# Attention weights transposed on DVE and by DMA through DRAM, in place of TensorE

## The chip, the cores and the metric

The kernel runs on one core of a Trainium2 chip. The metric is the device time of one execution in microseconds. Besides it the profile gives the span, from the first to the last instruction of the profiled execution.

The engines are named as in the profile: PE is TensorE's matmul, PEld its weight load, DVE is VectorE, ACT ScalarE, POOL GpSimd, and SP the engine that issues nearly all DMAs (SPq in the rows). L345 is line 345 of the kernel before.

## The reference

Two layers, on 256 tokens of width 2048, all float32. Each layer normalises the input, projects it to queries, keys and values, and runs two groups of eight attention heads on it. Then come an output projection and an MLP of width 8192. Cut to what the change touches:

```python
# (A) differential heads, 8 of value width 128, global:
p = jax.nn.softmax(sc, axis=-1)
w = (p[:, :, 0] - lam * p[:, :, 1]).astype(v.dtype)
return jnp.einsum('bhqk,bkhe->bqhe', w, v)
# (B) neighbourhood heads, 8 of width 128, window of 4 rows x 16 columns on a 64-wide grid, with bias:
p = jax.nn.softmax(sc.reshape(b, h, GRID_W, kr * kc), axis=-1).reshape(b, h, GRID_W, kr, kc)
return jnp.einsum('bhcrj,brcjhd->bchd', p.astype(v.dtype), v_nb)
```

The kernel computes (B) densely, with a mask: for each head the weights are a matrix of 256 queries by 256 keys. Both kinds of head need it with the keys on the partitions, since the product with v sums over keys.

## The kernel before

The weights of the whole model are a stream of 384 slabs of 128 x 2048 numbers (1 MB), 192 a layer. The program walks through them in order. For each slab SP loads `raw` (three buffers). ACT then writes the rounded high half `whi`, and DVE the rest `wlo`, in two pieces of 1024 columns each (lines 154 and 155; four buffers of either, so two slabs). PE multiplies a slab in one of two ways. `block_product` (lines 177 to 179) does 24 matmuls of 512 columns. `wide_product` does 16 of 512 columns (line 204) and 16 of 256 (line 208).

Attention is laid between the slabs. A head is a Python generator that stands in a list of tasks; `yield n` gives way for n slabs, and `between_slabs` wakes it. This sets priorities; a scheduler then lays out each engine's order of instructions, and at run time each engine works through its list in order and waits on semaphores.

- `diff_head` (16 in the program): scores, maxima (line 388), exponentials on ACT (line 391), the weighted difference `wd` on DVE (line 400), two slabs' pause, four transposes on PE (line 345), a copy from PSUM on ACT (line 405), one slab's pause, product with v (line 353).
- `na_head` and `na_stages` (16): two wide products give q and k of one head, so a head is reached every two slabs. Then scores (lines 439 to 441), bias (line 444), maxima (line 448), exponentials (line 452), division by the sum (line 457), two slabs' pause, four transposes (line 345), a split of the result into high half on ACT (line 325) and rest on DVE (line 326), one slab's pause, product with v in six matmuls (lines 465 to 467). The neighbourhood heads of a layer are called head 0 to head 7 below.

Each of the 32 heads thus has four PE transposes of 128 x 128, against an identity matrix, into one PSUM tile of the tag `tp` (two buffers). All slab loads go to SP in program order (line 71).

Of the kernel before, what the change touches and what calls it, by code (L numbers as in the profile page):

```python
# [12 lines left out]
F32 = mybir.dt.float32  # L13
F32R = mybir.dt.float32r
AF = mybir.ActivationFunctionType
# [4 lines left out]
P = 128  # L20
D = 2048
S = 256
NT = S // P
# [13 lines left out]
NB = 512  # L37
NEG = -1.0e30
IDLE = 9
RUN = 5 * RPB_C + GRID_W  # L40

RPB_FIRST = RPB_HEAD - 1 - (10 * RPB_C + GRID_W - 1 + WIN_C - 1)
# [8 lines left out]
def body(ctx, tc, x, x_t, w, gains_in, gains_o, final_g, lam_in, rpb, ident_in, rope_in, mask_in, out):  # L51
    nc = tc.nc
# [3 lines left out]
    work = ctx.enter_context(tc.tile_pool(name="work", bufs=2))  # L56
    small = ctx.enter_context(tc.tile_pool(name="small", bufs=4))
    ps = ctx.enter_context(tc.tile_pool(name="ps", bufs=2, space=PSUM))


    gin = const.tile([P, 2 * DEPTH, NK], F32, name="gin")
# [4 lines left out]
    go = const.tile([P, DEPTH, HEADS + 1], F32, name="go")  # L66
    xs = [const.tile([P, D], F32, name=f"x{t}") for t in range(NT)]

    def stream(dst, src):

        tc.keep_in_program_order(nc.sync.dma_start(dst, src))

    lam_sb = [None]

# [56 lines left out]
            between_slabs()  # L131


    slab_no = [0]
    x_rest = [None]

    def next_slab():
# [199 lines left out]
        nc.scalar.activation(rb, pb, AF.Copy)  # L337
        return rb

    def transposed_weights(pr):  # L340

        pw = ps.tile([P, NT, S], F32, name="tp", tag="tp", bufs=2)
        for t in range(NT):
            for kt in range(NT):
                nc.tensor.transpose(pw[:, kt, t * P:(t + 1) * P], pr[:, t, kt * P:(kt + 1) * P], ident)  # L345
        return pw

    def weights_times_v(wt, v, j):

# [26 lines left out]
    def diff_head(q, k, vs, j, nlam, gsub, put):  # L376

        neg = small.tile([P, 2, NT], F32, name="neg")
        sm = small.tile([P, 2, NT], F32, name="sm")
        pr = []  # L380
        sc = [ps.tile([P, NT, S], F32, name="sc", tag="sc", bufs=2) for _ in range(2)]
        for t in range(NT):
            for m in range(2):
                both = q[m][:, j, t * P:(t + 1) * P]
                nc.tensor.matmul(sc[m][:, t, :], both, k[m][:, j, :], start=True, stop=False)  # L385
                nc.tensor.matmul(sc[m][:, t, :], both, k[2 + m][:, j, :], start=False, stop=True)  # L386
        for m in range(2):
            nc.vector.tensor_reduce(neg[:, m, :], sc[m], axis=AX.X, op=ALU.max, negate=True)
            p = work.tile([P, NT, S], F32, name="pr", tag="pr", bufs=3)
            for t in range(NT):  # L390
                nc.scalar.activation(p[:, t, :], sc[m][:, t, :], AF.Exp, bias=neg[:, m, t:t + 1],
                                     accum_out=sm[:, m, t:t + 1])
            pr.append(p)
        rs = small.tile([P, 2, NT], F32, name="rs")
        nc.vector.reciprocal(rs, sm)
        c = small.tile([P, NT], F32, name="c")
        nc.vector.scalar_tensor_tensor(c, sm[:, 0, :], nlam, rs[:, 1, :], op0=ALU.mult, op1=ALU.mult)
        wd = work.tile([P, NT, S], F32, name="wd", tag="wd")
        for t in range(NT):
            nc.vector.scalar_tensor_tensor(wd[:, t, :], pr[1][:, t, :], c[:, t:t + 1], pr[0][:, t, :],  # L400
                                           op0=ALU.mult, op1=ALU.add)
        yield 2
        pw = transposed_weights(wd)
        wt = work.tile([P, NT, S], F32, name="wT", tag="wT", bufs=3)
        nc.scalar.activation(wt, pw, AF.Copy)
        yield 1
        po = weights_times_v(wt, vs[0], j)
        ss = small.tile([P, NT], F32, name="sso")
        for t in range(NT):
            junk = work.tile([P, HD], F32, name="junk", tag="junk", bufs=1)  # L410
            nc.scalar.activation(junk, po[:, t, :], AF.Square, scale=rs[:, 0, t:t + 1],
                                 accum_out=ss[:, t:t + 1])
        r = rms_scale(ss, NT, HD)
        comb = small.tile([P, NT], F32, name="comb")
        nc.gpsimd.tensor_tensor(comb, r, rs[:, 0, :], op=ALU.mult)
        o = work.tile([P, NT, HD], F32, name="o", tag="o", bufs=4)
        for t in range(NT):
            nc.vector.tensor_scalar(o[:, t, :], po[:, t, :], comb[:, t:t + 1], None, op0=ALU.mult)
        yield 2
        put(to_mix(o, gsub))  # L420
# [14 lines left out]
    def na_stages(h, q, k, v, rq, bias, gain, sq_sum, put):  # L435
        sc = ps.tile([P, NT, S], F32, name="sc", tag="sc", bufs=2)
        for t in range(NT):
            ts = slice(t * P, (t + 1) * P)
            nc.tensor.matmul(sc[:, t, :], q[0][:, ts], k[0], start=True, stop=False)  # L439
            nc.tensor.matmul(sc[:, t, :], q[1][:, ts], k[0], start=False, stop=False)  # L440
            nc.tensor.matmul(sc[:, t, :], q[0][:, ts], k[1], start=False, stop=True)
        sb = work.tile([P, NT, S], F32, name="wd", tag="wd")
        for t in range(NT):
            nc.vector.scalar_tensor_tensor(sb[:, t, :], sc[:, t, :], rq[t],
                                           bias[:, 2 - 2 * t:6 - 2 * t, :].rearrange("p a b -> p (a b)"),
                                           op0=ALU.mult, op1=ALU.add)
        neg = small.tile([P, NT], F32, name="neg")
        nc.vector.tensor_reduce(neg, sb, axis=AX.X, op=ALU.max, negate=True)
        pr = work.tile([P, NT, S], F32, name="pr", tag="pr", bufs=3)
        sm = small.tile([P, NT], F32, name="sm")  # L450
        for t in range(NT):
            nc.scalar.activation(pr[:, t, :], sb[:, t, :], AF.Exp, bias=neg[:, t:t + 1],
                                 accum_out=sm[:, t:t + 1])
        rs = small.tile([P, NT], F32, name="rs")
        nc.vector.reciprocal(rs, sm)
        for t in range(NT):
            nc.scalar.activation(pr[:, t, :], pr[:, t, :], AF.Copy, scale=rs[:, t:t + 1])
        yield 2
        wt = split_plain(transposed_weights(pr), [P, NT, S], "wT", 3)
        yield 1  # L460
        po = ps.tile([P, S], F32, name="tp", tag="tp", bufs=2)
        j = h % 4
        for kt in range(NT):
            vh, vl = (part[:, kt, j * HD:(j + 1) * HD] for part in v)
            nc.tensor.matmul(po, vh, wt[0][:, kt, :], start=kt == 0, stop=False)  # L465
            nc.tensor.matmul(po, vl, wt[0][:, kt, :], start=False, stop=False)  # L466
            nc.tensor.matmul(po, vh, wt[1][:, kt, :], start=False, stop=kt == NT - 1)
        if h == 0:
            nc.scalar.activation(sq_sum, po, AF.Square)
        else:  # L470
            sq = work.tile([P, S], F32, name="sq", tag="o", bufs=4)
            nc.scalar.activation(sq, po, AF.Square)
            nc.gpsimd.tensor_tensor(sq_sum, sq_sum, sq, op=ALU.add)
        put(split_mix(po, gain))
# [225 lines left out]
```

## Time and profile before

| | us |
|---|---|
| median of 3 runs (2220.17 to 2221.09) | 2220.28 |
| the profiled execution | 2220.29 |
| its span | 2218.5 |
| PE busy | 2206.3 |
| PEld busy | 1884.7 |
| DVE busy | 1371.9 |
| ACT busy | 1121.7 |
| POOL busy | 91.7 |

An engine's busy time is the time in which it had an instruction under way. Matmuls overlap each other on PE, so what an instruction costs is read from the distance between starts rather than from its own length. Between the profiled execution and its span lie 1.8 us.

### The profile page before, as it was taken

What the parts mean: (1) busy time and instruction counts of PE and PEld (TensorE: products, weight loads), DVE (VectorE), ACT (ScalarE), POOL (GpSimd) and SP (SyncE); (2) the same over time, 40 slices, a digit from 0 to 9 for tenths busy, and PEclk for the clock granted to TensorE, in tenths of its full rate; (3) what the DMA queues carried; (4) which work ended last, traced back from release to release, by engine and by line L of the source; (5) the groups of instructions that cost most, each with busy time, mean ns of one, the idle gap of its engine ahead of it and who ended that gap; (6) DMA issues with size and microseconds to landing.
All of it is one profiled execution on the core that took longest, in us unless ns stands there. A gap on an engine that the chain in (4) does not pass through costs nothing.

```text
span 2218.5 us, 28803 instructions
## 1 busy us (share of the span) xinstructions
PE 2206.3 (99%) x11298; PEld 1884.7 (85%) x11298; DVE 1371.9 (62%) x1777; ACT 1121.7 (51%) x1677; POOL 91.7 (4%) x136
## 2 busy tenths in 40 slices
PE   9999999999999999999999999999999999999998
PEld 7888888888888888888888888888888888888886
DVE  7776765664565565565567767666655655655654
ACT  6665664544453454454456666545434434544543
POOL 1110110000000000000011101000000000000000
PEclk9999999999999999999999999999999999999999
DMA  9444445455555555555654444554555555555553
GB/s 330 172 171 163 163 168 182 180 189 192 196 190 191 201 188 190 192 190 190 199 180 168 171 166 158 189 186 178 189 193 198 188 192 194 190 190 190 190 190 133
DMA packets 61431, 414.31 MB, mean 187 GB/s; under 512 B 7024, under 2 KB 9328, under 8 KB 12144
## 3 DMA queue, kind: packets, MB, share of 16 engines
q1 hardware_dynamic: 60864, 411.40, 51.9%
q8 instruction: 88, 1.44, 0.3%
q10 hardware_dynamic: 432, 1.08, 0.1%
q14 instruction: 47, 0.39, 0.1%
HBM read 410.35 MB, written 2.10 MB: 186 GB/s over the span
## 4 chain that ended last, share of the span: by engine, by line
PE 99%; DMA 0%; ACT 0%; DVE 0%; POOL 0%; SPq 0%; issue 0%; ACTq 0%; POOLq 0%
PE accw L204 26%; PE acc L177 18%; PE acc L178 18%; PE acc L179 18%; PE accw L208 14%; PE tp L353 1%; PE tp L345 1%; PE tp L252 0%; PE sc L386 0%; PE sc L385 0%; PE tp L292 0%; DMA xT<-in_x_t 0%; PE tp L466 0%; PE sc L440 0%; PE tp L465 0%; PE sc L439 0%
## 5 line engine op out<-in xcount | busy, mean ns | idle before, releaser
L155 DVE TENSOR_TENSOR wlo<-raw,whi 128x1024 fp32r<-128x1024 f32 (+1 forms) x772 | 931.8, 1225 | 594.0 <-ACT whi L154 442.1
L154 ACT ACTIVATE whi<-raw 128x1024 fp32r<-128x1024 f32 (+1 forms) x772 | 813.5, 1055 | 855.4 <-PE acc L178 557.8
L204 PE MATMUL accw<-hT,whi 128*128 128x512 f32 x2560 | 614.1, 391 | 0.0
L204 PEld LDWEIGHTS accw<-hT,whi 128*128 128x128 f32 x2560 | 469.8, 188 | 90.5
L178 PE MATMUL acc<-whi,u2T 128*128 128x512 f32 x1024 | 399.0, 390 | 0.0
L177 PE MATMUL acc<-whi,u2T 128*128 128x512 f32 x1024 | 398.6, 389 | 0.0
L179 PE MATMUL acc<-wlo,u2T 128*128 128x512 f32 x1024 | 398.3, 389 | 0.0
L208 PEld LDWEIGHTS accw<-hT,wlo 128*128 128x128 f32 x2560 | 328.5, 191 | 12.5
L208 PE MATMUL accw<-hT,wlo 128*128 128x256 f32 x2560 | 332.4, 283 | 0.0
L179 PEld LDWEIGHTS acc<-wlo,u2T 128*128 128x128 f32 x1024 | 192.3, 188 | 39.8
L177 PEld LDWEIGHTS acc<-whi,u2T 128*128 128x128 f32 x1024 | 192.3, 188 | 39.5
L178 PEld LDWEIGHTS acc<-whi,u2T 128*128 128x128 f32 x1024 | 192.3, 188 | 39.3
L177 PE MATMUL acc<-whi,hT 128*128 128x512 f32 x512 | 201.6, 394 | 2.0 <-ACT whi L154 2.0
L178 PE MATMUL acc<-whi,hT 128*128 128x512 f32 x512 | 201.2, 393 | 0.0
L179 PE MATMUL acc<-wlo,hT 128*128 128x512 f32 x512 | 197.7, 392 | 0.0
L161 DVE SCALAR_TENSOR_TENSOR u2T<-u,u2T 128x256 fp32r<-128x256 f32 x128 | 54.3, 424 | 123.2 <-ACT u2T L160 123.2
L211 ACT ACTIVATE low<-accw 128x256 f32<-128x256 f32 x160 | 61.0, 381 | 124.3 <-PE accw L208 124.3
L177 PEld LDWEIGHTS acc<-whi,hT 128*128 128x128 f32 x512 | 96.3, 188 | 21.1 <-ACT whi L154 2.7
L179 PEld LDWEIGHTS acc<-wlo,hT 128*128 128x128 f32 x512 | 96.1, 188 | 19.3
L178 PEld LDWEIGHTS acc<-whi,hT 128*128 128x128 f32 x512 | 96.3, 188 | 18.4
L177 PE MATMUL acc<-whi,mix 128*128 128x512 f32 x256 | 101.0, 395 | 0.0
L178 PE MATMUL acc<-whi,mix 128*128 128x512 f32 x256 | 100.3, 392 | 0.0
(119 smaller groups left out, 1349.3 us busy)
## 6 DMA issues: line engine op xcount, KB each, us to landing
raw<-in_w SPq DMA_DIRECT2D x382, 1024.0 KB, 4.8
x<-in_x SPq DMA_DIRECT2D x2, 1024.0 KB, 11.2
out<-xg SPq DMA_DIRECT2D x8, 256.0 KB, 3.1
table<-in_rpb SPq DMA_DIRECT2D x4, 438.0 KB, 11.8
xT<-in_x_t SPq DMA_DIRECT2D x3, 512.0 KB, 8.6
raw<-in_w SPq DMA_DIRECT2D x4, 256.0 KB, 5.4
raw<-in_w SPq DMA_DIRECT2D x2, 512.0 KB, 7.6
gb<-in_final_g ACTq DMA_DIRECT2D x2, 512.0 KB, 4.4
```

Of the source, the lines that this page charges most:

```text
L154: nc.scalar.activation(hi[:, c:c + step], r, AF.Copy)
L155: nc.vector.tensor_sub(lo[:, c:c + step], r, hi[:, c:c + step].bitcast(F32))
L161: nc.vector.scalar_tensor_tensor(dst_lo, src, scale, dst_hi.bitcast(F32), op0=ALU.mult, op1=ALU.subtract)
L177: nc.tensor.matmul(acc[t], ah, wh, start=k == 0, stop=False)
L178: nc.tensor.matmul(acc[t], al, wh, start=False, stop=False)
L179: nc.tensor.matmul(acc[t], ah, wl, start=False, stop=k == n_k - 1)
L204: nc.tensor.matmul(acc, hi[:, (k % 8) * P:(k % 8 + 1) * P], h_t[k].rearrange("p a b -> p (a b)"), start=k == 0, stop=False)
L208: nc.tensor.matmul(acc[:, :S], lo[:, (k % 8) * P:(k % 8 + 1) * P], h_t[k][:, 0], start=False, stop=k == NK - 1)
L211: nc.scalar.activation(low, acc[:, S:], AF.Copy)
L345: nc.tensor.transpose(pw[:, kt, t * P:(t + 1) * P], pr[:, t, kt * P:(kt + 1) * P], ident)
L353: nc.tensor.matmul(po[:, t, :], wt[:, kt, t * P:(t + 1) * P], v[:, kt, j * HD:(j + 1) * HD], start=kt == 0, stop=kt == NT - 1)
```

## The change

The transposes leave PE. DVE's transpose instruction transposes each 32 x 32 square of the 128 x 512 tile within its own 32 partitions, into `sqt`. One DMA writes `sqt` to a DRAM tile `way` (256 KB). Four DMAs read it back into `moved`, each 64 KB: load `a` takes, for the 32 queries of one square row, four runs of 128 numbers (512 bytes) from each of the 32 rows and puts them on 4 x 32 partitions. The result has the keys on the partitions, and the query squares in the order a, t, u (which of four squares in a half, which half of the queries, which half of the keys).

The differential heads put this in order with two ACT copies (in place of one copy from PSUM). The neighbourhood heads split it as it lies, and PE reads the moving operand in runs of 32 numbers. A pause of one slab stands between the DVE transpose and the DMAs. Slab loads after the eighth are no longer held in program order. The tags change: `sqt` 2 buffers, `way` 4, `moved` 2, and `wT` or its two halves 2.

```diff
     def stream(dst, src):
 
-        tc.keep_in_program_order(nc.sync.dma_start(dst, src))
+        load = nc.sync.dma_start(dst, src)
+        if slab_no[0] < 8:
+            tc.keep_in_program_order(load)
...
-    def transposed_weights(pr):
-
-        pw = ps.tile([P, NT, S], F32, name="tp", tag="tp", bufs=2)
-        for t in range(NT):
-            for kt in range(NT):
-                nc.tensor.transpose(pw[:, kt, t * P:(t + 1) * P], pr[:, t, kt * P:(kt + 1) * P], ident)
-        return pw
+    def squares_transposed(pr):
+
+
+        sq = work.tile([P, NB // SQ // 4, NT, NT, SQ], F32, name="sqt", tag="sqt", bufs=2)
+        nc.vector.transpose(sq.rearrange("p b t u j -> p (t u) b j"),
+                            pr.rearrange("p t (u b j) -> p (t u) b j", u=NT, j=SQ))
+        return sq
+
+    def squares_moved(sq):
+
+
+        way = dram.tile([P, NB], F32, name="way", tag="way", bufs=4)
+        nc.sync.dma_start(way, sq.rearrange("p b t u j -> p (b t u j)"))
+        wt = work.tile([P, P // SQ, NT, NT, SQ], F32, name="moved", tag="wT", bufs=2)
+        for a in range(P // SQ):
+            nc.sync.dma_start(wt[:, a].rearrange("p t u j -> p (t u j)"),
+                              way[a * SQ:(a + 1) * SQ].rearrange("i (b e) -> b i e", b=P // SQ))
+        return wt
...
+        sq = squares_transposed(wd)
+        yield 1
+        moved = squares_moved(sq)
         yield 2
-        pw = transposed_weights(wd)
-        wt = work.tile([P, NT, S], F32, name="wT", tag="wT", bufs=3)
-        nc.scalar.activation(wt, pw, AF.Copy)
+        wt = work.tile([P, NT, S], F32, name="wT", tag="wTs", bufs=2)
+        for t in range(NT):
+            nc.scalar.activation(wt[:, :, t * P:(t + 1) * P].rearrange("p u (a j) -> p a u j", j=SQ),
+                                 moved[:, :, t], AF.Copy)
         yield 1
...
+        sq = squares_transposed(pr)
+        yield 1
+        moved = squares_moved(sq)
         yield 2
-        wt = split_plain(transposed_weights(pr), [P, NT, S], "wT", 3)
+        wt = split_plain(moved, [P, P // SQ, NT, NT, SQ], "wTs", 2)
         yield 1
...
-            nc.tensor.matmul(po, vh, wt[0][:, kt, :], start=kt == 0, stop=False)
-            nc.tensor.matmul(po, vl, wt[0][:, kt, :], start=False, stop=False)
-            nc.tensor.matmul(po, vh, wt[1][:, kt, :], start=False, stop=kt == NT - 1)
+            wh, wl = (part[:, :, :, kt, :].rearrange("p a t j -> p t a j") for part in wt)
+            nc.tensor.matmul(po, vh, wh, start=kt == 0, stop=False)
+            nc.tensor.matmul(po, vl, wh, start=False, stop=False)
+            nc.tensor.matmul(po, vh, wl, start=False, stop=kt == NT - 1)
```

How the change moves instructions is shown at three places, all among the neighbourhood heads of the first layer. Lines of the changed kernel are a little higher than those of before (L154 there is L159, L204 is L209, L325 is L330, L457 is L477, L465 is L489).

On PE before, at the end of a slab (line 208), the four transposes of head 4 stand ahead of the scores of head 5:

```order
L208 MATMUL accw<-hT,wlo 128x256 x16
L345 MATMUL tp<-ident,pr 128x128 x4
L439 MATMUL sc<-half 128x256
L440 MATMUL sc<-half 128x256
L441 MATMUL sc<-half 128x256
```

On PE after the change, at the end of that same slab (counting from 0 it is slab 46), stands the product with v of head 4 (L489 to L491, whose two `half` are the split weights):

```order
L209 MATMUL accw<-hT,whi 128x512 x16
L213 MATMUL accw<-hT,wlo 128x256 x16
L489 MATMUL tp<-half,vs 128x256
L490 MATMUL tp<-half,vs 128x256
L209 MATMUL accw<-hT,whi 128x512 x6
L491 MATMUL tp<-half,vs 128x256
L489 MATMUL tp<-half,vs 128x256
```

No transpose is left there; the product has moved back by one slab, to where the transposes stood.

On ACT before, the split of head 2's weights (`half_2554`, read from the PSUM tile `tp_2549`), then the exponentials and the division of head 3 (`pr_2570`):

```order
L325 ACTIVATE half_2554<-tp_2549 128x512
L325 ACTIVATE half_2544<-whole_2542 128x256
L154 ACTIVATE whi_2728<-raw_2726 128x1024
L452 ACTIVATE pr_2570,sm_2571<-wd_2565,neg_2568 128x256 x2
L154 ACTIVATE whi_2732<-raw_2726 128x1024
L457 ACTIVATE pr_2570<-pr_2570,rs_2574 128x256 x2
```

On ACT after the change, the split of head 2 (now read from `moved_2539`, the tile that the DMAs fill) and the division of head 3 (`pr_2620`):

```order
L330 ACTIVATE half_2684<-moved_2539 128x512
L159 ACTIVATE whi_2849<-raw_2847 128x1024
L472 ACTIVATE pr_2620,sm_2621<-wd_2615,neg_2618 128x256 x2
L159 ACTIVATE whi_2853<-raw_2847 128x1024
L330 ACTIVATE half_2678<-kr_2595 128x256
L477 ACTIVATE pr_2620<-pr_2620,rs_2624 128x256 x2
```

And a little further on, still on ACT after the change, the split of head 3 (`moved_2690`) and the division of head 4 (`pr_2772`):

```order
L472 ACTIVATE pr_2772,sm_2773<-wd_2767,neg_2770 128x256 x2
L159 ACTIVATE whi_3000<-raw_2998 128x1024
L330 ACTIVATE half_2836<-moved_2690 128x512
L477 ACTIVATE pr_2772<-pr_2772,rs_2776 128x256 x2
L159 ACTIVATE whi_3004<-raw_2998 128x1024
```

What moved: the split of a head, which waited for PE before, now waits for DMAs, and it stands ahead of the division by which the next head's weights become ready.

On SP before, the loads of the whole program are slabs, but for a few constants and the bias tables (`table`):

```order
L71 DMA lam_sb<-in_lam_in 128x512
L71 DMA go<-in_gains_o 128x18
L71 DMA negmask<-in_mask_in 128x64
L71 DMA table<-in_rpb 64x8x219 x2
L71 DMA raw<-in_w 128x2048 x185
L71 DMA table<-in_rpb 64x8x219 x2
```

On SP after the change, heads 3 and 4 (`sqt_2628` and `sqt_2780`) between the slabs:

```order
L75 DMA raw_3085<-in_w 128x2048
L357 DMA way_2688<-sqt_2628 128x512
L360 DMA moved_2690<-way_2688 128x1x128 x4
L75 DMA raw_3152<-in_w 128x2048
L357 DMA way_2840<-sqt_2780 128x512
L75 DMA raw_3220<-in_w 128x2048
L360 DMA moved_2842<-way_2840 128x1x128 x4
L75 DMA table_9596<-in_rpb 64x8x219
```

Five DMAs a head now stand in SP's list. At some heads a slab's load lies between the write of `way` and the four reads, at others not; the second layer's bias table has moved up into the first layer.

## Rows read from the trace of the kernel before

**Rows 1.** The page's parts 1 (busy time) and 4 (chain that ended last).
```profile
PE 2206.3 (99%) x11298; PEld 1884.7 (85%) x11298; DVE 1371.9 (62%) x1777; ACT 1121.7 (51%) x1677; POOL 91.7 (4%) x136
...
PE 99%; DMA 0%; ACT 0%; DVE 0%; POOL 0%; SPq 0%; issue 0%; ACTq 0%; POOLq 0%
```

**Rows 2.** Waits of all engines: us in total, times, longest us.
```profile
ACT whi L154 <- PE acc L178: 557.8, 350, 2.4
...
ACT whi L154 <- DMA raw<-in_w: 3.2, 3, 1.6
```

**Rows 3.** Groups by line, PE: xcount | busy us, mean ns of one | idle before.
```profile
L345 PE MATMUL tp<-ident,wd 128*128 128x128 f32 x64 | 9.9, 272 | 0.0
...
L345 PE MATMUL tp<-ident,pr 128*128 128x128 f32 x64 | 9.6, 272 | 0.0
```

**Rows 4.** Timeline of PE, heads 3 to 5, first layer: start us, us, instructions.
```profile
281.21 3.80 PE L204 MATMUL accw<-hT,whi 128*128 128x512 f32 x16
...
286.76 0.60 PE L345 MATMUL tp<-ident,pr 128*128 128x128 f32 x4
...
287.32 0.28 PE L440 MATMUL sc<-half 128*128 128x256 f32 x1
287.44 0.28 PE L441 MATMUL sc<-half 128*128 128x256 f32 x1
...
294.19 3.80 PE L204 MATMUL accw<-hT,whi 128*128 128x512 f32 x16
...
299.74 0.49 PE L345 MATMUL tp<-ident,pr 128*128 128x128 f32 x3
```

**Rows 5.** Timeline: slabs 26 and 37 on DVE, slab 27 on PE.
```profile
159.91 1.23 DVE L155 TENSOR_TENSOR wlo<-raw,whi 128x1024 fp32r<-128x1024 f32 x1 [0.26 <-ACT whi L154]
...
175.55 0.39 PE L177 MATMUL acc<-whi,hT 128*128 128x512 f32 x1
...
228.52 2.36 DVE L155 TENSOR_TENSOR wlo<-raw,whi 128x1024 fp32r<-128x1024 f32 x2 [0.49 <-PE accw L208]
```

**Rows 6.** Groups by line, ACT and DVE: xcount | busy us, mean ns of one.
```profile
L154 ACT ACTIVATE whi<-raw 128x1024 fp32r<-128x1024 f32 (+1 forms) x772 | 813.5, 1055 | 855.4 <-PE acc L178 557.8 <-PE accw L204 268.7 <-issue 13.4
...
L211 ACT ACTIVATE low<-accw 128x256 f32<-128x256 f32 x160 | 61.0, 381 | 124.3 <-PE accw L208 124.3
...
L452 ACT ACTIVATE pr<-wd,neg 128x256 f32<-128x256 f32 x32 | 16.0, 500 | 0.3
L457 ACT ACTIVATE pr<-pr,rs 128x256 f32<-128x256 f32 x32 | 14.4, 496 | 0.8 <-DVE rs L455 0.8
...
L448 DVE TENSOR_REDUCE neg<-wd 128x2 f32<-128x512 f32 x16 | 10.8, 677 | 0.1
...
L325 ACT ACTIVATE half<-tp 128x512 fp32r<-128x512 f32 x16 | 9.5, 593 | 0.6
...
L325 ACT ACTIVATE half<-kr 128x256 fp32r<-128x256 f32 x16 | 6.4, 401 | 1.6 <-DVE kr L426 1.6
L452 ACT ACTIVATION_READ_ACCUMULATOR pr<-wd,neg 128x1 f32 x32 | 6.0, 186 | 0.0
```

**Rows 7.** DMA queue (packets, MB, share) and issues: KB each, median us to landing.
```profile
q1 hardware_dynamic: 60864, 411.40, 51.9%
...
raw<-in_w SPq DMA_DIRECT2D x382, 1024.0 KB, 4.8
...
out<-xg SPq DMA_DIRECT2D x8, 256.0 KB, 3.1
table<-in_rpb SPq DMA_DIRECT2D x4, 438.0 KB, 11.8
...
xT<-in_x_t SPq DMA_DIRECT2D x1, 128.0 KB, 2.5
ident<-in_ident_in SPq DMA_DIRECT2D x1, 64.0 KB, 7.6
```

**Rows 8.** Tile `table`, its loads on SP: ns of an issue, min/median/max.
```profile
L71 SPq DMA_DIRECT2D table<-in_rpb x4: 596/622/714, 26.1 to 1084.4; - x4
```

More of the change, by code (lines that the diff above doesn't have):

```diff
@@ L39 @@
 IDLE = 9
+SQ = 32
 RUN = 5 * RPB_C + GRID_W
@@ L58, in body @@
     ps = ctx.enter_context(tc.tile_pool(name="ps", bufs=2, space=PSUM))
+    dram = ctx.enter_context(tc.tile_pool(name="dram", bufs=4, space=bass.MemoryType.DRAM))
     gin = const.tile([P, 2 * DEPTH, NK], F32, name="gin")
@@ L67, in body @@
     xs = [const.tile([P, D], F32, name=f"x{t}") for t in range(NT)]
+    slab_no = [0]
     def stream(dst, src):
-        tc.keep_in_program_order(nc.sync.dma_start(dst, src))
+        load = nc.sync.dma_start(dst, src)
+        if slab_no[0] < 8:
+            tc.keep_in_program_order(load)
     lam_sb = [None]
@@ L131, in finish_tasks @@
             between_slabs()
-    slab_no = [0]
     x_rest = [None]
```

## The prediction

> **What bounds the kernel now.** I read the page's busy times and the chain that ended last first [rows 1]. PE is busy for 2206.3 of the 2218.5 us of the span and makes 99% of the chain, DMA 0%. A share near 100% can still hide an engine that is slow at its own work, so the waits come next [rows 2]: ACT, which prepares the weights, stands idle 557.8 us in 350 waits until PE has finished with a buffer, and only 3.2 us for a slab that has not arrived. The stream of weights runs ahead of PE, so PE is the bound. What leaves PE leaves the time, one for one, as long as PE finds nothing new to wait for. The rest of the work is about that condition.
>
> **What is removed.** There are 64 transposes of `wd` and 64 of `pr` [rows 3]. Their busy time, 9.9 + 9.6 = 19.5 us, counts overlaps twice, so I take the distance between starts [rows 4]. From the start of four transposes (286.76) to the start of L440 (287.32) is 0.56 us, and L440 to L441 shows that a matmul of 256 columns takes 0.12. (L439, which stands between them in the program, has no row of its own here; it gets 0.12 as well.) Four transposes therefore cost 0.56 - 0.12 = 0.44 us, and 32 heads 32 x 0.44 = 14.1 us. Against the profiled execution's 2220.29, which is the median to within 0.01, that makes **2206.2**, if all else is hidden. The busy time, 19.5, is the gain's upper end: 2200.8.
>
> **What is added beside PE.** DVE gets 32 transposes of 128 x 512. No row shows one. The nearest is the reduction over the same 512 numbers, 0.68 us [rows 6]; I take 0.7, with twice that as the upper bound, together 22 to 45 us on an engine that is idle 38% of the span [rows 1]. A bound from below, nothing, would change no result. ACT's differential copy becomes two (at most 0.4 us each [rows 6], before one of about 0.6), the neighbourhood split keeps its size. Both are small against ACT's 557.8 us of waiting. Without that cover they would cost at most 32 x 0.7 = 22 us. PE now reads the neighbourhood weights in runs of 32. Between nothing and double the time for each of the 16 x 6 matmuls, 96 x 0.12 = 11.5 us, I take nothing: no row shows an operand read in such runs, so none speaks for a loss and none excludes it; it is rival C. The DMAs add 32 x 0.5 MB, 16.8 MB to 411.4 [rows 7], at a mean load of 51.9%. The issues cost 0.62 us each [rows 8], 3.1 us a head on SP, where the wait for `way` also holds the slab loads behind it. A slab lands in 4.8 us [rows 7], and heads are two slabs apart, so both together leave SP free over half the 12.98 us between two wide products [rows 4].
>
> At one place the notes speak against the change. The Trainium skill ("VectorE: DVE Perf Modes", The three transpose paths) says that DVE transposes only 32 x 32 blocks, and sends a full 128 x 128 one to TensorE. No run here has yet timed the alternative; here TensorE is the engine that bounds, which the rule does not weigh, and the sum by it would be no gain at all, 2220.
>
> **The new wait.** Call C the time from the end of the DVE transpose to the last landing of `moved`. It has three parts. `way`, 256 KB, lands in 3.1 us as `out` does, or 4.8 behind a slab. Three more issues follow the first read, 3 x 0.62 = 1.9. The last read, 64 KB, lands in 2.5 (`xT`, 128 KB), 4.8 (a slab), or 7.6 (`ident`, the same 64 KB, at the start of the program); 11.8 is the extreme (`table`) [rows 7, 8]. The lower end is 3.1 + 1.9 + 2.5 = 7.5, the upper 4.8 + 1.9 + 7.6 = 14.3, with the table's landing 18.5. I take one leg behind a slab and the other like `out`: 4.8 + 1.9 + 3.1 = 9.8, and 0.1 for each of three hand-overs (an estimate, from the 0.26 and 0.49 us that DVE waited for ACT and PE in [rows 5]): **C = 10.1**.
>
> Differential heads. The tightest is the first of the second block. DVE ends slab 26 at 159.91 + 1.23 = 161.1, the transpose 161.8, and PE reaches the product with v, ahead of slab 27's end, at 175.55 [rows 5]. Less 0.8 for the two copies, C may be 13.0. These are covered at 10.1.
>
> Neighbourhood heads. The order shows a ring that was not there before: on ACT the split of head h, which waits for `moved`, stands ahead of the division of head h + 1, without which that head's transpose and DMAs cannot begin. If C is long, the heads follow each other at C plus ACT's and DVE's work between, and no longer at PE's pace. That work, from [rows 6], with 0.59 for the split, 0.38 `low`, 0.69 an exponential with its accumulator, 1.06 a `whi`, 0.40 the half of k, about 0.9 to 1.0 the two divisions, 0.7 the transpose:
> head 0 to 1: split, low, divisions, transpose: 2.6; 1 to 2: split, low, two exponentials, whi, divisions, transpose: 5.0; 2 to 3: split, two whi, two exponentials, half, divisions, transpose: 6.1; 3 to 4: split, divisions, transpose: 2.2. Together 15.9.
> Head 0's transpose ends at 228.52 + 2.36 + 0.7 = 231.6, behind the two `wlo` of slab 37 [rows 5]. Head 4's product can start after five times C: 231.6 + 15.9 + 5C + 0.6 for its own split = 248.1 + 5C. On PE it stands where head 4's neighbour had its transposes, at 299.74 [rows 4], less five groups of 0.44 saved on the way: 297.5. So the ring is hidden up to **C = 9.9**, and each us beyond it costs 5 us a layer; the loop ends with the eighth head, whose limit I find about the same. At my C of 10.1 it gives back 1.0 us a layer: 2206.2 + 2.0 = **2208.2**. Behind the waiting split stand ACT's `whi` and, on DVE, `wlo` of the next slabs: they are the way by which a late head would stop PE.
>
> **Rivals.** *The trip through DRAM sets the pace (A).* The same sum with a longer C: the whole gain is gone at (14.1 / 2) / 5 = 1.4 us over the limit, C = 11.3, and beyond that the kernel is slower. At 14.3 it is 2206.2 + 2 x 5 x 4.4 = 2250. For it speaks that `ident` needed 7.6 us for 64 KB and that SP's list puts a slab's load between at some heads; against it that DMA is idle half the time and that `out` and `xT` landed in 3.1 and 2.5.
>
> *The reads are narrow (B).* Each read has a slowest dimension of four runs. If only four of the 16 DMA engines carry it, those four must move 128 packets a head besides their share of two slabs, 51.9% of 12.98 = 6.7 us. Two slabs take 12.98 - 0.44 = 12.5 us without the transposes, so the stream follows those four once the packets take over 12.5 - 6.7 = 5.8 us a head, 45 ns each; below that nothing is lost. By bytes, 51.9% x 2218.5 x 16 / 411.4 = 44.8 engine-us a MB [rows 1, 7], a head's 64 KB an engine is 2.9 us and hidden; by packets, 51.9% x 2218.5 x 16 / 60864 = 0.30 us each, it is 38.7 and ruinous. Packets of 512 bytes are much nearer the first price. With 10 us it would be about 2206.2 + 16 x (10 + 6.7 - 12.5) = 2273. The Trainium skill ("DMA: Bandwidth & Descriptors", Why a DMA increments its semaphore by 16 and not by 1) says that the number of engines is the largest one up to 16 that divides the slowest dimensions of both patterns, which here is 4; no run here shows it yet.
>
> *Reading runs of 32 slows PE (C):* 2206.2 + 11.5 = 2217.7, no difference to be told. *The transposes cost their busy time (D):* 2200.8.
>
> **How the numbers follow.** The ring's limit about met, as forecast, 0.55, itself from 2203 to 2214 (0.44 is read to 0.05 a group, and C to 0.8 on the far side). A 0.24: about 0.06 of it still faster, 0.07 with no difference, 0.11 slower. B slower 0.12, C 0.05, D 0.04. A measurement here can tell about 0.2%, 4.4 us, from no change. Faster: 0.55 + 0.06 + 0.04 = 0.65; same: 0.07 + 0.05 = 0.12; slower: 0.11 + 0.12 = 0.23. I predict the likeliest, 2208. From 2202 to 2236 the range leaves out D (0.04) and what of A and B lies beyond C = 12.9, some 0.15.
>
> **What would show it.** Right: no transposes on PE, PE busy down by 14 to 20 us, PE still 99% of the chain, `moved` landing soon enough that `split <- DMA moved` waits on ACT stay hidden, SP waiting for `way` some 3 to 5 us a head without slabs coming late. Ring: in the neighbourhood heads PE waits for the ACT half of the weights or for a `whi`, ACT waits for DMA `moved`, and the time between two wide products is over 12.5 us there and nowhere else. B: long DMA landings of `moved` and of the slabs beside it, and ACT waiting for `raw`. C: L489 to L491 at more than 0.12 from start to start. The prediction is wrong above all if C is over 11.3, since each us of it counts ten times.

## The result, and the profile after

The changed kernel takes 2254.96 us (median of 4 runs, 2247.02 to 2261.40) against 2220.41 for the kernel before: slower, ratio 1.0153, 95% interval 1.0118 to 1.0189. The forecast was 2208, range 2202 to 2236. The profiled execution took 2258.09 us, its span 2256.3.

The page's parts 1 (busy time) and 4 (chain that ended last) of the changed kernel, to be held against [rows 1]:

```profile
PE 2209.9 (98%) x11170; PEld 1880.2 (83%) x11170; DVE 1390.4 (62%) x1809; ACT 1111.4 (49%) x1693; POOL 109.4 (5%) x136
...
PE 83%; DMA 9%; DVE 2%; ACT 2%; SPq 2%; issue 1%; POOL 0%; ACTq 0%; POOLq 0%; DVEq 0%
```

PE has 128 matmuls fewer and yet is busy 3.6 us longer; the chain, 99% PE before, runs through DMA for 9%. The waits of all engines (us in total, times, longest), with [rows 2] as their counterpart:

```profile
ACT whi L159 <- PE acc L183: 495.6, 307, 2.3
...
ACT half L330 <- DMA moved<-way: 87.4, 16, 10.3
ACT wT L424 <- DMA moved<-way: 83.1, 16, 9.0
...
PE tp L489 <- ACT half L330: 23.3, 11, 4.7
...
PE tp L297 <- DVE rs L411: 7.1, 2, 4.2
...
ACT whi L159 <- DMA raw<-in_w: 2.3, 2, 1.7
```

ACT waits for `moved` at each of the 32 heads, 170 us in all, and PE for ACT's half of the weights, 23.3 us. The slabs are as punctual as before (2.3 us against 3.2). All of the added time lies in the two attention stretches; elsewhere slabs follow each other as before.

A neighbourhood head on the timeline (start, us, instruction, the idle time before it and what ended it), head 3 of the first layer:

```profile
293.52 0.63 ACT L330 ACTIVATE half<-moved 128x512 fp32r<-128x512 f32 x1 [6.62 <-DMA moved<-way]
294.06 0.89 ACT L477 ACTIVATE pr<-pr,rs 128x256 f32<-128x256 f32 x2
...
294.20 0.39 PE L489 MATMUL tp<-half,vs 128*128 128x256 f32 x1 [2.82 <-ACT half L330]
...
294.98 0.71 DVE L349 STREAM_TRANSPOSE sqt<-pr 128x512 f32<-128x512 f32 x1
...
295.72 0.33 SPq L357 DMA_DIRECT2D way<-sqt  x1
```

This is the ring of the prediction: ACT stands 6.62 us before head 3's split, and only after it come head 4's division, transpose and DMA. PE waits 2.8 us for head 3's product with v.

A differential head has another victim, which the prediction had not named:

```profile
113.86 0.42 ACT L424 ACTIVATE wT<-moved 128x256 f32<-128x256 f32 x1 [6.55 <-DMA moved<-way]
...
114.19 0.35 ACT L431 ACTIVATE junk<-tp,rs 128x128 f32<-128x128 f32 x1
...
115.37 0.19 POOL L225 TENSOR_SCALAR v<-sso 128x2 f32<-128x2 f32 x1 [5.77 <-ACT junk L431]
...
116.65 0.61 DVE L438 TENSOR_SCALAR o<-tp,comb 128x128 f32<-128x128 f32 x2 [3.25 <-POOL comb L435]
...
117.41 0.63 PE L297 MATMUL tp<-ident,nat 128*128 128x128 f32 x4 [2.87 <-DVE rs L411]
...
118.58 0.63 PE L184 MATMUL acc<-wlo,hT 128*128 128x512 f32 x1
```

Behind ACT's wait for `moved` stand the sums of squares (`junk`) of the head before. POOL's scale and DVE's `o` follow them, and until `o` is made, the PSUM tile `tp` of that head isn't free, for which PE's next transposes (L297) wait. (The row names `rs`, DVE's next instruction, because it ended last. By the semaphores PE's wait was over at 117.355: after DVE's signal for `o` at 117.275, before the one for `rs` at 117.358.) The last row shows a third thing: a matmul of 512 columns takes 0.63 us there. The windows (stretch, its length, busy time of PE, PEld, DVE, ACT and POOL, granted clock, DMA share, GB/s) say why:

```profile
117.00:123.00 6.00, 5.59 (x20) 4.55 (x21) 5.80 (x11) 4.60 (x8) 0.00 (x0) 0.72 0.15 56
...
337.00:344.50 7.50, 6.78 (x20) 5.63 (x21) 4.61 (x6) 6.00 (x12) 0.64 (x1) 0.54 0.26 61
...
700.00:760.00 60.00, 60.00 (x266) 49.68 (x265) 31.28 (x29) 23.34 (x22) 0.00 (x0) 1.00 0.55 193
```

After a wait of some us PE's granted clock falls to one half (1.2 in place of 2.4 GHz) for 3.4 or 6.8 us. The clock's records show five such stretches in the attention, 27.3 us together, so about 13.7 us of lost time; one more, at the end of the program, is in every kernel here and isn't counted. The sum closes: 2204.6 (the span without any wait, first experiment) + 37.5 us of waits between PE's matmuls + 13.7 = 2255.8, against 2256.3.

How the trip is made up is read from the DMA issues and from the records of their landings, mean us of the 16 neighbourhood heads, changed kernel and wide reads (second experiment):

```
                    way lands   four issues   last read lands   C
changed kernel         4.8          1.7             5.4         12.1
wide reads             5.1          1.4             3.2          9.8
```

A read's semaphore rises in 5 steps in the changed kernel; those of all other DMAs rise in 16. The first of the five comes 0.9 to 1.0 us after a head's first read is issued, at every head before the first 512-byte packet starts (1.3 us or later). So it tells of no data, and four landings are left.

### The profile page after: what moved, and what is told of

It reads as the page before. It is cut to its first block, busy times and chain, and to the rows that moved or that the text cites. A ratio compares the mean times of both kernels' runs of the same rounds, so it can differ in the third digit from the quotient of the medians.

```text
span 2256.3 us, 28878 instructions
## 1 busy us (share of the span) xinstructions
PE 2209.9 (98%) x11170; PEld 1880.2 (83%) x11170; DVE 1390.4 (62%) x1809; ACT 1111.4 (49%) x1693; POOL 109.4 (5%) x136
## 4 chain that ended last, share of the span: by engine, by line
PE 83%; DMA 9%; DVE 2%; ACT 2%; SPq 2%; issue 1%; POOL 0%; ACTq 0%; POOLq 0%; DVEq 0%
PE accw L209 22%; PE acc L182 16%; PE acc L184 16%; PE acc L183 16%; PE accw L213 11%; DMA moved<-way 5%; DMA way<-sqt 4%; SPq L360 1%; DVE wlo L160 1%; DVE sqt L349 1%; ACT whi L159 1%; PE tp L257 0%; ACT pr L407 0%; PE tp L297 0%; ACT pr L477 0%
## 5 line engine op out<-in xcount | busy, mean ns | idle before, releaser
L159 ACT ACTIVATE whi<-raw 128x1024 fp32r<-128x1024 f32 (+1 forms) x772 | 809.8, 1054 | 757.9 <-PE acc L183 495.6
L209 PE MATMUL accw<-hT,whi 128*128 128x512 f32 x2560 | 616.5, 391 | 0.1
L209 PEld LDWEIGHTS accw<-hT,whi 128*128 128x128 f32 x2560 | 469.2, 188 | 90.6 <-ACT whi L159 0.5
L166 DVE SCALAR_TENSOR_TENSOR u2T<-u,u2T 128x256 fp32r<-128x256 f32 x128 | 54.4, 425 | 123.0 <-ACT u2T L165 123.0
L182 PE MATMUL acc<-whi,mix 128*128 128x512 f32 x256 | 102.1, 399 | 0.0
L184 PE MATMUL acc<-wlo,mix 128*128 128x512 f32 x256 | 101.9, 398 | 0.0
```

Source lines behind the costliest of these rows:

```text
L159: nc.scalar.activation(hi[:, c:c + step], r, AF.Copy)
L166: nc.vector.scalar_tensor_tensor(dst_lo, src, scale, dst_hi.bitcast(F32), op0=ALU.mult, op1=ALU.subtract)
L182: nc.tensor.matmul(acc[t], ah, wh, start=k == 0, stop=False)
L184: nc.tensor.matmul(acc[t], ah, wl, start=False, stop=k == n_k - 1)
L209: nc.tensor.matmul(acc, hi[:, (k % 8) * P:(k % 8 + 1) * P], h_t[k].rearrange("p a b -> p (a b)"), start=k == 0, stop=False)
```

## The experiments

**Theory 1** when the experiments began: the trip is longer than forecast; ACT takes its instructions in order, and what stands behind its wait for `moved` makes PE wait. Rivals: the engines pay for their new work; the added traffic, on few DMA engines, is itself the cost. The table at the end of this section has all runs.

**No trip.**

```diff
-        way = dram.tile([P, NB], F32, name="way", tag="way", bufs=4)
...
-        return wt
+        return sq
```

> Leaves out the trip through DRAM: the split and the copies read sqt itself (four buffers), so the weights are transposed only within their squares. PE, ACT and DVE do the same work as in the changed kernel. Theory 1 (the whole loss is ACT waiting for moved, and what stands behind it in ACT's order): 2206 us, 2204 to 2209, no PE wait over 1 us among the heads and no stretch at the low clock. Rival (the engines pay: DVE's transposes, two copies, PE reading runs of 32): 2212 or more, up to 2218.

Measured: 2206.74 (2206.48 to 2208.91), no PE wait and no low clock among the heads. The gain of the change, 14.0 us, is what the prediction worked out, and the new work of DVE, ACT and PE costs nothing. The whole loss is the trip's.

**Wide reads.**

```diff
-        for a in range(P // SQ):
-            nc.sync.dma_start(wt[:, a].rearrange("p t u j -> p (t u j)"),
-                              way[a * SQ:(a + 1) * SQ].rearrange("i (b e) -> b i e", b=P // SQ))
+        for b in range(P // SQ):
+            nc.sync.dma_start(wt[b * SQ:(b + 1) * SQ].rearrange("p a t u j -> p a (t u j)"),
+                              way.rearrange("(a i) (b e) -> b i a e", i=SQ, b=P // SQ)[b])
```

> The four reads of way are cut by key square instead of by query square, so that each goes from 128 rows to 32 partitions and its slowest dimension is 32 instead of 4; same bytes, same 512-byte runs. If four engines carried each read before (5 landings on its semaphore, where others have 16), it now counts more landings, and the median landing of a read falls from 4.6 to about 3 us. Theory 1: the time from transpose to last landing falls by 1.6, the ring gives back 5 x 1.6 a layer and the differential heads some: 2230 to 2242. Rival (the narrow reads are no part of it; the order in which they queue behind slabs is): landing and time as before, 2250 to 2260.

Measured: 2216.49 (2209.82 to 2218.78, 10 runs). Each read's semaphore now rises in 16 steps, and the median landing falls from 4.6 to 2.6 us. The trace agrees with the rule of the Trainium skill that the prediction cited for rival B ("DMA: Bandwidth & Descriptors", Why a DMA increments its semaphore by 16 and not by 1): four landings for a slowest dimension of 4, sixteen for 32. The gain, 38.5 us, is larger than Theory 1 had it: the five C of heads 0 to 4 add up to 44.1 and 49.4 us in the two layers, just below the limit of 5 x 9.9 = 49.5, and the differential heads' waits are gone altogether, with the low clock there.

```profile
ACT half L330 <- DMA moved<-way: 49.0, 16, 8.7
ACT wT L424 <- DMA moved<-way: 37.6, 15, 5.5
...
PE tp L489 <- ACT half L330: 5.2, 3, 4.0
```

These are its waits: ACT still waits for `moved`, half as long, and PE hardly notices.

**One kind of head at a time.** `transposed_weights` is put back for the heads named:

```diff
-        sq = squares_transposed(wd)
-        yield 1
-        moved = squares_moved(sq)
         yield 2
+        pw = transposed_weights(wd)
```

> Differential heads transposed on PE as in the kernel before; neighbourhood heads as changed. In the changed kernel PE waits 12.6 us at differential heads, and 10.2 us at half clock there cost 5.1 more; putting 64 transposes back costs 7.0. Theory 1, losses local to their heads: 2255 - 17.7 + 7.0 = 2244. Rival (the neighbourhood heads' ring is the whole cost, and waits at differential heads only move it earlier): 2255 + 7 = 2262. Rival (the differential heads start the delays of the others): under 2235.

> Neighbourhood heads transposed on PE as in the kernel before (with two buffers for the halves); differential heads as changed. In the changed kernel PE waits 25.0 us at neighbourhood heads, and 17.1 us at half clock there cost 8.5 more; 64 transposes back cost 7.0. Theory 1: 2255 - 33.5 + 7.0 = 2228.5, that is, still slower than before, by the differential heads alone. As predicted (differential heads are covered): 2213.

Measured: 2244.87 and 2231.31, both as Theory 1 has it. The losses are local to their heads. The second run is clear against the prediction, by which the differential heads cost nothing.

The first run also repeats the test of the ring. The five C of heads 0 to 4 add up to 54.7 and 54.4 us in its two layers; over the limit of 5 x 9.9 that makes 5.2 and 4.9. PE waited 5.1 and 4.9 up to head 4's product. In the changed kernel the sums are 54.5 and 54.7, so 5.0 and 5.2; PE waited 5.6 and 5.2.

**Sums of squares on DVE.** Line 431's squares on ACT become a scaling, a product and a sum on DVE.

> Narrow reads as in the changed kernel; the differential heads' sums of squares (junk, line 431) go from ACT to DVE as six short instructions a head, so that ACT's wait for the next head's moved no longer stands ahead of them. Theory 1 (late sums of squares hold the PSUM tile tp, for which PE's next transposes wait): most of the 12.6 us of waits and 5.1 us of half clock at differential heads go, 2238; up to 2247 if DVE's wlo, which wait for ACT's whi behind the same copy, hold the squares up in turn. Rival (it is the product with v that is late): no change, 2255.

Measured: 2251.02 (2248.35 to 2260.11). In the profiled execution the differential heads' waits fall from 12.5 to 6.8 us and their low clock from 10.2 us to none, so they lose 10.8 us less. But that execution is the fastest of four. The median is above the range, and 3.9 us below the changed kernel's it doesn't stand clear of the spread of either. Nor did the edit change one thing alone: the neighbourhood heads lose about as much as before (23.9 us of waits), yet ACT's order is another there (the split of heads 0 to 2 now stands behind the next head's division), and the mean C of heads 0 to 4 is 13.3 and 12.9 us in the two layers, where it was 10.9. The run fits the mechanism and doesn't show its size.

**A later split.**

```diff
-        yield 2
+        yield 3
         wt = split_plain(moved, [P, P // SQ, NT, NT, SQ], "wTs", 2)
```

> Narrow reads as in the changed kernel; in the neighbourhood heads the pause ahead of the split is three slabs instead of two, so PE's product with v stands a slab later. The trip and the ring on ACT stay as they are. Theory 1 (five links of C plus 15.9 us must end before head 4's product is due): the due time moves back by 6 us, the limit from 9.9 to 11.1, the measured mean of 11.0 is about covered, and the waits at the ends of the layers go too: 2255 - 33.5 = 2221.5, 2218 to 2232. Rival (the delayed whi and wlo behind the split stop PE, whatever the product waits for): 2250 or more.

Measured: 2246.43. Theory 1 missed. In the neighbourhood heads PE now waits mostly for scores: 11.8 us in four places, 5.6 of them in one, for the halves of q and k, which stand behind the split on ACT; for the products it waits 3.3 us. The trip grew too, to a mean C of 12.8 and 13.4 in heads 0 to 4. A later due time doesn't help as long as the rest of ACT's work is queued behind the wait.

**Eight and sixteen wide reads** (the same loop with smaller pieces), and **one read** after four writes that put the squares in order.

> Wide reads, but eight of 32 KB instead of four of 64 KB: the same bytes, packets and engines; only four more issues, 4 x 0.43 us measured from start to start, so C is 1.5 to 2 us longer than in the wide kernel, about 11 in the first five links. Theory 1 (the length of the trip alone decides): 2228 to 2242, most of what the wide reads gained is lost again. Rival (narrow reads cost by holding up four engines, not by their length): as the wide kernel, 2214 to 2220.

> Wide reads in sixteen pieces of 16 KB: the same bytes and packets as in the wide kernel, but sixteen issues, at 0.43 to 0.45 us from start to start. C in the first five neighbourhood links: way 4.7, issues 6.6, last landing 1.8, together 13 instead of 9.4. Theory 1 (C decides): five links are 3 us each over the limit, 15 us a layer, plus waits at differential heads as in the changed kernel or more, plus half clock: 2250 to 2275. Rival (only narrow reads cost, by what they hold up on four engines): 2212 to 2222. If SP's issues make the slabs late, ACT waits for raw and not for moved.

> The squares are put in order on the way out: four writes of way, each from 32 partitions in runs of 512 bytes, and one read of 256 KB in rows of 2 KB, sixteen engines on both legs. As many DMAs as before, but PE's and ACT's waits hang on one landing: C about 1.7 for the issues, 2 to 5 for the last write, 2.5 to 4 for the read, 7 to 9. Theory 1: below both limits, as the wide kernel or a little better, 2208 to 2216.

Measured: 2212.11, 2231.05 and, in a single run, 2221.21: all three outside what Theory 1 said. The mean C of heads 0 to 4 in the two layers was 9.5 and 10.2, 16.4 and 16.4, 8.2 and 8.6. A longer trip cost less, and a shorter one more, than the formula. What differs beside C is the order of ACT's instructions: the scheduler lays the program out anew for each kernel, and with sixteen reads it put the split of heads 0 to 5 behind the division of the next head (with eight at two of seven places), with one read ahead even of the next head's exponentials. So the formula can be held to one order only; that the order is the whole difference was not tested. With sixteen reads the slabs come late too, 21.4 us for ACT in 15 waits:

```profile
ACT whi L159 <- DMA raw<-in_w: 21.4, 15, 3.6
```

**Both pauses longer**, with wide and with narrow reads.

> Wide reads, and three slabs' pause instead of two ahead of the split or copies in both kinds of head. Theory 1: the waits left in the wide kernel (5.7 us, two of three at the last head of a layer) and its half clock go: 2207 to 2210, near the kernel without the trip, 2206.7. Rival: a later product delays the last heads into the output projection, 2216 or more.

> Narrow reads with three slabs' pause in both kinds of head: the wide kernel with the longer pause took 2208.3, so this is the same kernel but for the width of its reads. Theory 1, as it stands after the run with the longer pause in neighbourhood heads alone (2246.4; the queries' and keys' halves behind ACT's wait then stop PE): the longer pause doesn't help narrow reads, 2235 to 2255. Rival (a longer pause is enough at any width): 2208 to 2215.

Measured: 2208.25 (2207.80 to 2208.47) and 2238.54. The pause is worth 8 us with wide reads and 16 with narrow ones, but only the width makes the kernel faster than before.

**What reads `moved` on POOL.** The copies and both halves of the split are POOL instructions; narrow reads.

> Narrow reads as in the changed kernel; whatever reads moved goes to POOL: the differential copies and both halves of the neighbourhood split. No ACT or DVE instruction waits for the trip any more. Theory 1 (the price is paid by what stands behind ACT's wait): the waits at neighbourhood heads (25.0 us and 8.5 of half clock) go, 2222; some of those at differential heads may stay, since POOL's scale factors (L225 to L435) now stand behind its copies: 2208 to 2230. Rival (PE's product with v is itself late, on whatever engine the split is): 2245 or more; POOL's copies of 128 x 512 have no row yet and add to this if they take over 3 us.

Measured: 2225.30 (2220.31 to 2232.31). With the wait taken off ACT, the differential heads lose nothing any more, and the neighbourhood heads 11.8 us of waits and 5.1 by the clock. That confirms the queue behind ACT's wait as a cause: the reads are as narrow as ever, and the mean C of heads 0 to 4 is even longer, 14.5 and 14.1. POOL's two halves take 0.79 and 1.61 us, longer than ACT's and DVE's 0.63 and 0.69, and PE's products wait for them.

**The ring cut alone**, with narrow and with wide reads:

```diff
-            nc.scalar.activation(pr[:, t, :], pr[:, t, :], AF.Copy, scale=rs[:, t:t + 1])
+            tc.keep_in_program_order(nc.scalar.activation(pr[:, t, :], pr[:, t, :], AF.Copy, scale=rs[:, t:t + 1]))
...
-        wt = split_plain(moved, [P, P // SQ, NT, NT, SQ], "wTs", 2)
+        wt = [work.tile([P, P // SQ, NT, NT, SQ], F32R, name="half", tag="wTs", bufs=2) for _ in range(2)]
+        tc.keep_in_program_order(nc.scalar.activation(wt[0], moved, AF.Copy))
+        nc.vector.tensor_sub(wt[1], moved, wt[0].bitcast(F32))
```

> The changed kernel, narrow reads and all, with one thing held: on ACT the division of head h + 1 and the split of head h stay in the order in which the program writes them, division first. The ring is cut; trip, products on PE and differential heads are as in the changed kernel. Theory 1 (the ring carries the delay from head to head): the waits at neighbourhood heads (25.0 us, and 8.5 of half clock) go but for the last heads of a layer, where the order hardly changes (at most 4.9 us twice and some half clock): 2222 to 2234. Rival (each trip of 12 us is late by itself): 2245 or more.

> Wide reads and the division held first. Theory 1: as the wide kernel (2216.5), less what the ring left there (0.9 us of waits and some at the last heads): 2208 to 2214. Rival (holding an order costs ACT something of its own): 2216 or more.

Measured with narrow reads: 2245.46 (2239.84 to 2251.66). By the number the rival held, but not because trips of 12 us are late. The products of heads 0 to 4 of the first layer follow each other at PE's pace, 12.6 to 12.8 us apart, without any wait of PE; but the trip grows from head to head. The landings, in us from the issue, of `way`, of the slab that is issued behind the four reads (the first and the last of its 16 steps), and of `way` with wide reads:

```
head                          0     1     2     3     4
narrow: way                  5.5   6.3   7.6   8.4   9.0
narrow: slab, first step     4.6   4.7   4.6   4.8   4.8
narrow: slab, last step      6.4   7.7   7.9   7.6  10.4
wide:   way                  5.4   5.0   5.2   5.8   5.2
```

Twelve of the slab's 16 steps come within 0.7 us of the first; the last four are late, as if the engines that carry the reads took the slab later than the others. `way`, issued behind two slabs, lands 0.9 us later with each head.

The delay isn't a queue that the engines carry from head to head. Each time `way` of these heads lands, they stand empty, because SP issues nothing while it waits for `way` (two rows of SP, start and length; then two windows as above, the next to last number the DMA share):

```profile
259.61 0.33 SPq L357 DMA_DIRECT2D way<-sqt  x1
267.23 2.27 SPq L360 DMA_DIRECT2D moved<-way  x4
...
255.50:257.00 1.50, 1.50 (x14) 1.50 (x13) 0.56 (x2) 1.50 (x5) 0.00 (x0) 1.00 0.28 79
266.60:268.70 2.10, 2.10 (x14) 1.79 (x13) 1.46 (x4) 2.10 (x8) 1.57 (x2) 1.00 0.03 11
```

In the first window only reads are under way, and a share of 0.28 is 4.5 of 16 engines; in the second `way` lands (267.21), at a share of 0.03. SP's list is thus a second ring: `way`, its landing, four reads, two slabs, the next `way`. From landing to landing of `way` it took 12.4, 13.4, 13.4 and 13.6 us in the first layer and 12.4, 13.5, 13.3 and 13.2 in the second, on average more than PE's 12.6 a head. This is read from the trace; no run took the trip off SP's list.

At head 5, where the two loads of the bias table also stand ahead of `way`, C is 24.4 us, and PE stands:

```profile
322.42 0.63 ACT L483 ACTIVATE half<-moved 128x512 fp32r<-128x512 f32 x1 [7.65 <-DMA moved<-way]
...
323.10 0.58 PE L491 MATMUL tp<-half,vs 128*128 128x256 f32 x1 [6.21 <-ACT half L483]
```

With wide reads: 2207.33 us (2206.67 to 2207.52), ratio 0.9939 (0.9924 to 0.9954), the fastest kernel here that leaves nothing out. Its page and its waits:

```profile
PE 2192.8 (99%) x11170; PEld 1871.7 (85%) x11170; DVE 1391.3 (63%) x1809; ACT 1119.5 (51%) x1693; POOL 96.5 (4%) x136
...
PE 99%; DMA 0%; ACT 0%; DVE 0%; POOL 0%; SPq 0%; issue 0%; ACTq 0%; POOLq 0%
```

```profile
ACT wT L424 <- DMA moved<-way: 37.5, 14, 5.8
...
ACT half L483 <- DMA moved<-way: 12.9, 4, 4.5
```

No row of PE waiting for a head is left; it gives back 13.5 of the 14.1 us.

All runs, from the traces: PE's waits between matmuls in the differential (d) and the neighbourhood (n) stretch, us at half clock there, and the sum 2204.6 + waits + half of the us at half clock (+ 7.05 where 64 transposes are back on PE), beside the measured span.

```
                        waits d   n    half clock d   n     sum     span
changed kernel            12.5  25.1      10.2     17.1   2255.8  2256.3
no trip                    0     0         0        0     2204.6  2204.6
wide reads                 0     5.7       0        3.4   2212.0  2213.5
differential on PE         0    21.0       0       17.1   2241.2  2243.0
neighbourhood on PE       13.3   0         6.8      0     2228.3  2230.4
squares on DVE             6.8  23.9       0       17.1   2243.9  2246.6
narrow, split later        9.6  16.9       6.8     13.7   2241.3  2242.8
wide, eight reads          0     4.0       0        0     2208.6  2210.3
wide, both later           0     0         0        0     2204.6  2206.4
split on POOL              0    11.8       0       10.2   2221.5  2222.9
wide, sixteen reads        6.2  12.2       3.4      6.8   2228.1  2230.3
one read                   0     9.8       0        6.8   2217.8  2219.4
narrow, both later        11.7  11.4       0        3.4   2229.4  2233.1
narrow, division first    13.9  13.9      10.2     13.7   2244.4  2244.8
wide, division first       0     0         0        0     2204.6  2204.8
```

The sum, in which only waits of over 0.35 us are counted, stays 0 to 4 us below the span in all fifteen.

## Why the prediction was wrong

**Gain, 14.1 us: right.** Without the trip the kernel gains 14.0, with a trip that is hidden 13.5. The busy-time end (19.5) and rival C (11.5 us for operands in runs of 32) are out.

**Added work beside PE: right.** DVE's transpose takes 0.71 us, where 0.7 was taken from a reduction:

```profile
L349 DVE STREAM_TRANSPOSE sqt<-pr 128x512 f32<-128x512 f32 x16 | 11.3, 707 | 1.5 <-ACT pr L477 1.2
```

**C = 10.1: the step that failed first.** Of its three parts, `way` (4.8) and the issues (1.9) measured 4.8 and 1.7 us. The landing of the last read, sized like `out` at 3.1, measured 5.4, and C 12.1 (10.9 in heads 0 to 4, on which the forecast rests). The semaphore of `out` rises in 16 steps, that of a read in 5. The text had the narrow reads as rival B and priced them only by what they take from the stream; their own landing, which is a part of C, was left at the wide price. With wide reads the last landing is 3.2 and C 9.8, near the forecast 10.1, and the time 2216.5: slower than the forecast 2208, but in its range.

C alone doesn't make the miss. With 10.9 in place of 10.1 the prediction's own sum gives 2206.2 + 10 x 1.0 = 2216. The other 39 us are terms that it took for equal or put at nothing: the last heads, the differential heads and the clock.

**The ring and its limit of 9.9: right, for the order of that kernel.** The formula gives the waits up to head 4 to 0.6 us in four layers. It describes that kernel and is no remedy: with this ring cut the reads were still narrow, and the time fell by 9.5 us only, within the spread of the runs. What the prediction took for equal, the last heads, was not: C is 11.8 and 17.5 us at heads 5 and 6 of the first layer (9.4 at head 7), 12.6, 14.9 and 17.4 at heads 5 to 7 of the second, and they add 5.8 and 8.4 us of waits.

**Differential heads covered up to C = 13.0: wrong.** The deadline was that of the product with v. The first to be late are the sums of squares of the head before, queued behind the copy on ACT, which hold a PSUM tile. At C of 9 to 13 the differential heads had 12.5 us of waits. That the sums of squares are the reason is read from the trace; the run that moved them to DVE left it open how much they account for.

**The clock: missing.** Waits were priced at their length. 27.3 us at half clock add about 13.7 us, over a third of the waits themselves.

**Rivals.** A is what happened, with the last heads, the differential heads and the clock on top of its sum. B was judged by its price for a packet: 128 packets of 512 bytes, 30 ns each in the trace, are 3.8 us a head, under its limit of 5.8. By that the four engines keep up, and they do: they were empty at each landing of `way`. B's price left out that SP, waiting for `way`, lets them stand empty, so that the reads lengthen each turn of its list (13.2 to 13.6 us in six of eight turns, with the ring on ACT cut). The prediction had SP "free over half the 12.98 us". In the changed kernel itself this doesn't show, since the ring on ACT spaces the heads out.

Open stay how much of a turn on SP's list is packets and how much waiting, what the trip would cost if another engine issued it, the spread of the changed kernel's runs (14 us, where the wide kernel with the division first has 0.9), and what share of the wide kernel's gain comes from the shorter landing and what from the shorter turn.

## What to carry to other kernels

When work leaves the bounding engine for a path with a DMA, the price is not in the path's busy time but in the queue behind the instruction that waits for it: list what stands there, whom it feeds, and which buffers it holds, and add the low clock that can follow PE's waits. Size a DMA's landing by a row with the same shape, above all the same slowest dimension; turning the loop over the pieces by 90 degrees, with no byte more or less, was worth 38 us here. Where a scheduler lays the program out again for each edit, look at its order first before a difference between two kernels is put down to the edit.

## What the runs showed of the hardware

Narrow reads (slowest dimension 4) raised their semaphore in 5 steps, the first ahead of any packet, and landed in 4.6 us (median, changed kernel); wide ones (slowest dimension 32) in 16 steps and 2.6 us (first kernel with wide reads), with the same bytes and the same runs of 512 bytes. Pieces of 32 KB, wide, landed in 1.8 us. A slab behind four narrow reads had its first step 4.6 to 4.8 us after its issue and its last after 6.4 to 10.4. PE reads a moving operand of 256 columns in runs of 32 numbers at the pace of a contiguous one, 0.12 us from start to start. PE's granted clock fell to one half after waits of about 2 to 6 us in these kernels and not after every one; in the kernels whose waits among the heads were all under 2 us it fell only at the end of the program.
